# A two-layer transformer with experts: the triangular inversion on one engine, and operand tiles at multiples of 256 bytes

## The chip, the cores and the metric

The kernel is one program on one core of a Trainium2 chip. The metric is device microseconds of that core. Three runs of the kernel before took 2130.3, 2129.33 and 2136.47 us (median 2130.3). Engines: TensorE (PE in rows; PEld its weight loads), VectorE (DVE), ScalarE (ACT), GpSimd (POOL), SyncE (SP), which only issues transfers here. SBUF is the on-chip memory: a tile is a range of bytes at the same start address in each of the 128 partitions. For a matmul the stationary operand (the weights) is loaded first and the moving operand then streams past it.

## The reference

Two layers over 256 context and 256 latent tokens of width 1024, float32. Layer 0 mixes by bidirectional retention and grouped-query attention and has a dense SwiGLU of width 2816. Layer 1 mixes by differential attention and a bidirectional RWKV-7 recurrence and has eight SwiGLU experts of width 3584, two per token. The heavy matrix products and the recurrence, cut to what matters:

```python
def swiglu(h, wg, wu, wd):
    return (jax.nn.silu(h @ wg) * (h @ wu)) @ wd

# experts, layer 1: top 2 of 8, every expert's three matrices are read whole
for e in range(N_EXPERTS):
    out = out + gates[..., e:e + 1] * swiglu(h, wg[e], wu[e], wd[e])

# RWKV-7, one direction, per token
s_new = (s * wt[:, :, None, :]
         + jnp.einsum('bhvk,bhk->bhv', s, at)[..., None] * bt[:, :, None, :]
         + vt[..., None] * kt[:, :, None, :])
y = jnp.einsum('bhvk,bhk->bhv', s if read_before else s_new, rt)
```

## The kernel before

**Split matmuls.** Every weight matrix arrives in float32 and is split into a high half (a copy on ScalarE that rounds to float32r) and a low half (a subtraction on VectorE). One product is then three matmuls: high with high, high with low, low with high (`mm3`, L266 to 269). The split of weights is `wsplit` (L262 and 263: `raw` to `whi`, `wlo`) in the attention and dense parts and `split_to` (L272 and 273: `mraw` to `mhi`, `mlo`) in the expert part, where each transfer brings 1 MB. In the experts' gate and up products (`g`, `u`) the token tiles `xh`, `xl` are stationary and the weights `mhi`, `mlo` move; in the experts' down product (`y`) `acts` is stationary. In the dense FFN gate and up (`acc<-hTh,whi`) the weights are stationary and the tokens `hTh`, `hTl` move; in the dense down product (`acc<-whi,ah`) the activations `ah`, `al` are stationary. In the projections in front of attention (`acc<-whi,hTh`) the tokens are stationary.

**RWKV.** Time is cut into chunks of 64; each chunk and head needs the inverse of a unit lower triangular 64x64 matrix, done as two 32x32 diagonal inversions (`inv_blocks`, `inv_diag`) and a joining product (`inv_join`). All heads and chunks of one half (256 tokens, both directions) go at once, one per partition and block. `inv_blocks` lets TensorE build the blocks (`dg`, `off`) from the tiles `AR` and `BK` that `prep` computes on VectorE and ScalarE, and transposes them to `M`. `inv_diag` goes through 31 steps; step t multiplies column t of `M` by row t of the growing inverse `N` into a scratch tile, and adds it to `N` in place. VectorE has the columns below a cut (2 in half 0, 8 in half 1) with the scratch `tmv`, GpSimd the rest with `tmg`. `inv_join` transposes `N` twice into `X0` and `X1`, copies eight blocks into `XF` and computes the off-diagonal block by `gp` and `wp` on TensorE. `chain` then carries the state through the chunks with `lm`, `z`, `u`, `s` on TensorE and small copies on VectorE and ScalarE between.

**Order.** `weave` interleaves the issue of two sequences of steps in a given proportion: half 0's inversion beside `prep` of half 1, and half 1's inversion and join beside `chain` of half 0. Each engine works through its instructions in the order issued. Tiles come from pools; a pool's tiles are laid one behind the other, so a small tile ahead of large ones sets the address of all that follow. Weight transfers are issued by SyncE as far ahead as the ring of raw buffers allows.

Of the kernel before, what the change touches and what calls it, by code (L numbers as in the profile page):

```python
# [8 lines left out]
F32 = mybir.dt.float32  # L9
F32R = mybir.dt.float32r  # L10
I32 = mybir.dt.int32
# [14 lines left out]
LAM_INIT = 0.8 - 0.6 * math.exp(-0.3)  # L26
C = 64
RAW = 8

CUT0, CUT1 = 2, 8  # L30

NM, N0 = 72, 0.1
M1, M3 = 15, 1
# [97 lines left out]
def _build(top, tc, nc, V, S, G, T, I, O):  # L131
# [4 lines left out]
    def open_right(key, name, bufs=1):  # L136
        cur[key] = ExitStack()
        return cur[key].enter_context(tc.tile_pool(name=name, bufs=bufs, side="right", reuse_waits="tile"))
# [25 lines left out]
    acc, tpp, att, ybank = (bank(k) for k in ("acc", "tp", "at", "y"))  # L164
    banks(acc=range(6), tp=(6, 7))
    cur["re"] = cur["ce"] = ExitStack()
    top.callback(lambda: [cur[k].close() for k in ("we", "xe", "me", "he", "re", "ce")])

    def const_(shape, name, dt=F32):
        return cp.tile(shape, dt, name=name)  # L170
# [1 line left out]
    def load_consts(pool, g, queue=nc.scalar):  # L172
        t = pool.tile([128, CST["cst_" + g].shape[1]], F32, name="cst_" + g)
        queue.dma_start(t, I["cst_" + g])

        def cc(k):
            o, n = COFF[k]
            return t[:, o:o + n]
        return cc

    cc = load_consts(cp, "all")
    ident = cc("ident")

    Xl = const_([128, 2, D], "Xl")
    cur["rb"] = 4
    hp = cur["h"] = open_right("he", "h")
    hT = tuple(hp.tile([128, 8, 512], F32R, name=n_) for n_ in ("hTh", "hTl"))
    open_mod()
# [9 lines left out]
    def columns(name, parts):  # L198
# [4 lines left out]
        for nm, src, k in parts:  # L203
# [9 lines left out]
    voff = {}  # L213
    cvec = columns("cvec", (("c", I["c"].rearrange("o (k p) -> (o k) p", p=128), 8),
                            ("cc", I["c_ctx"].rearrange("(k p) -> k p", p=128), 8)))
    cond = const_([128, 8, 32], "cond")
    V.memset(cond, 0.0)
    S.activation(cond[:, :, 0:2].rearrange("p k r -> p r k"), cvec.rearrange("p (r k) -> p r k", r=2), AF.Silu)

# [571 lines left out]
    def layer1():  # L791
# [11 lines left out]
        mu1 = rp.tile([128, 15], F32, name="mu1")  # L803
        muh = rp.tile([128, 15], F32, name="muh")
        ka1 = rp.tile([128, 4], F32, name="ka1")
        o = voff["mu"]
        V.tensor_scalar(mu1, vec[:, o:o + 15], -1.0, 1.0, op0=ALU.mult, op1=ALU.add)
        V.tensor_scalar(muh, vec[:, o:o + 15], 0.5, None, op0=ALU.mult)
# [5 lines left out]
        twd = rp.tile([128, 512], F32, name="twd")  # L814
        adT = rp.tile([128, 512], F32, name="adT")
        sgd = rp.tile([128, 256], F32, name="sgd")
        bon = rp.tile([128, 2, 8], F32, name="bon")
        G.memset(vT[:, :, 0:64], 0.0)
        pads = []
        for i in range(2):  # L820
            p = xq.tile([128, 2, 258], F32, name=f"spad{i}")
            G.memset(p, 0.0)
            pads.append(p)

        def shift(i, a, dst, segs):

# [52 lines left out]
        def operands(pool, half):  # L879
            w = 64 * (1 + half)  # L880
            for d in range(2):
                AR[d, half] = pool.tile([128, 4, 4, w], F32, name=f"AR{d}{half}", tag=f"AR{d}{half}")
                BK[d, half] = pool.tile([128, 4, 4, 2, 64], F32, name=f"BK{d}{half}", tag=f"BK{d}{half}")
                WC[d, half] = pool.tile([128, 4, 4], F32, name=f"WC{d}{half}")

        def lora_weights(d):

# [131 lines left out]
            iv[half] = M, Lo  # L1019
            yield  # L1020

        def inv_diag(half, cut):

            M, Lo = iv[half]
            N = bn("N")
            G.memset(flat(N), 0.0)
            G.memset(flat(N)[:, 0:1024:33], 1.0)
            for t in range(31):
                for eng, name, j0, j1 in ((V, "tmv", 0, cut), (G, "tmg", cut, 31)):
                    j1 = min(j1, t + 1)  # L1030
                    if j1 <= j0:
                        continue
                    tm = qI.tile([128, 256], F32, name=name, tag=name, bufs=2)
                    n, m = 31 - t, j1 - j0
                    tv = tm[:, 0:n * m].rearrange("p (i j) -> p i j", i=n)
                    Nv = N[:, t + 1:32, j0:j1]
                    eng.tensor_tensor(tv, M[:, t + 1:32, t:t + 1].to_broadcast([128, n, m]),
                                      N[:, t:t + 1, j0:j1].to_broadcast([128, n, m]), op=ALU.mult)
                    eng.tensor_tensor(Nv, Nv, tv, op=ALU.add)
                yield  # L1040
            iv[half] = N, Lo
            yield

        def inv_join(half):

            N, Lo = iv[half]
            X0, X1 = bn("X0"), bn("X1")
            V.transpose(X0.rearrange("p u c -> p c u"), N.rearrange("p r c -> p c r"))
            V.transpose(X1.rearrange("p u r -> p r u"), N)
            yield  # L1050
            xf, xt = (X0, X1), (X1, X0)
            xF = XF[half].rearrange("p d c a t -> p d (c a) t")
            for d in range(2):
                for x in range(4):
                    V.tensor_copy(xF[32 * x:32 * x + 32, d, :, 32 * (x % 2):32 * (x % 2) + 32],
                                  xt[d][32 * x:32 * x + 32, 16 * d:16 * d + 16])
            gp = acc("gp")
            Gs = qI.tile([128, 16, 32], F32, name="Gs", tag="Gs", bufs=1)
            for d in range(2):
                for u in range(16):  # L1060
                    for h in range(2):
                        i_, o_ = 64 * h + 32 * d, 64 * h + 32 * (1 - d)
                        T.matmul(gp[o_:o_ + 32, u * 32:u * 32 + 32], Lo[i_:i_ + 32, u], xf[d][i_:i_ + 32, 16 * d + u],
                                 start=True, stop=True, tile_position=(i_, o_))
            S.activation(flat(Gs), gp, AF.Copy)
            yield
            wp_ = acc("wp")
            for d in range(2):
                for u in range(16):
                    for h in range(2):  # L1070
                        o_, i_ = 64 * h + 32 * d, 64 * h + 32 * (1 - d)
                        T.matmul(wp_[o_:o_ + 32, u * 32:u * 32 + 32], Gs[i_:i_ + 32, u], xt[d][i_:i_ + 32, 16 * d + u],
                                 start=True, stop=True, tile_position=(i_, o_))
            for d in range(2):
                for h in range(2):
                    o_ = 64 * h + 32 * d
                    S.activation(xF[o_:o_ + 32, d, :, 32 * (1 - d):32 * (1 - d) + 32],
                                 wp_[o_:o_ + 32].rearrange("p (u t) -> p u t", u=16), AF.Copy)
            yield

        banks(acc=(3, 4, 5), at=(0, 1, 2))
        drain(inv_blocks(0))
        weave((seq(prep(0, 1), prep(1, 1), inv_blocks(1)), 19), (inv_diag(0, CUT0), 32))
        rk = q.tile([128, 4, 256], F32, name="rkT", tag="Ei", bufs=1)
        for p in range(4):
            V.scalar_tensor_tensor(rk[:, p], rT[:, p], vcol("rk", p), kT[:, p, 256:512], op0=ALU.mult, op1=ALU.mult)
# [128 lines left out]
                ops.update(nxt)  # L1215
                yield

        weave((chain(0), 16), (seq(inv_diag(1, CUT1), inv_join(1)), 32))
        eI.close()
        eC.close()  # L1220
        mh, ml = (qA.tile([128, 8, 256], F32R, name=n_, tag=t_) for n_, t_ in (("mixh", "BK00"), ("mixl", "BK10")))
# [231 lines left out]
    def moe():  # L1453
# [3 lines left out]
        top_e, mp = top_pool("moe")  # L1457
        mc = load_consts(mp, "moe", nc.sync)
        h2h = {}
        h2l = mp.tile([128, 2, D], F32R, name="h2l")  # L1460
        Ar, Br, rt, rb = cur["route"]
        sel = mp.tile([128, 2, NE], F32, name="sel")
        gts = mp.tile([128, 2, NE], F32, name="gts")
        slotv = mp.tile([128, 2, NE], F32, name="slotv")
        wg, wu, wd = I["moe_w_gate"][0], I["moe_w_up"][0], I["moe_w_down"][0]
        split = []

# [153 lines left out]
        def gate_weights():  # L1621
# [13 lines left out]
            V.tensor_copy(cnt, ct[:, 0:8])  # L1635
            V.tensor_reduce(cm_, ct[:, 0:8], axis=AX.X, op=ALU.max)
            V.tensor_copy(cmx, cm_)
        cnt = mp.tile([128, NE], I32, name="cnt")
        cmx = mp.tile([128, 1], I32, name="cmx")


        def gather(g, k2s=range(4)):
# [240 lines left out]
```

## Time and profile before

| what | value |
|---|---|
| median of three runs | 2130.3 us |
| profiled execution | 2132.66 us, span 2130.9 us |
| TensorE busy | 2038.5 us (96%), mean granted clock 0.973 |
| VectorE busy | 1646.4 us (77%) |
| ScalarE busy | 1210.4 us (57%) |
| GpSimd busy | 152.6 us (7%) |
| bytes moved | 494.00 MB, mean 232 GB/s |

The profile is of one execution. Busy time is the time in which an engine works on some instruction; TensorE's matmuls are pipelined, so that two of them overlap and their durations add up to more than its busy time. How closely matmuls follow each other is read from the distance of their starts. The granted clock is the share of full speed (2.4 GHz) at which TensorE was let run. The idle time in front of an instruction is put down to what released it.

### The profile page before, as it was taken

To read this page: it belongs to the slowest core of one execution; us is meant where nothing else is said; L and a number is where in the kernel's file an instruction comes from. 1 tells how busy PE (TensorE), PEld (TensorE's weight loads), DVE (VectorE), ACT (ScalarE), POOL (GpSimd) and SP (SyncE) were. 2 spreads that over 40 slices of the span, in tenths; PEclk is the share of its full clock that TensorE was granted. 3 is DMA by queue.
4 is the path that set the end of the run, shared out by engine and by line. 5 is a ranking of instruction groups with operands and counts; after the bars stand their busy time and mean duration, and the time that the engine had idled before them with its cause. 6 is when DMAs were issued, how large, how long until landed. Compare 5 with 4: busy or idle time off the path is not lost. (4 is left out here: it accounts for less than half of the span.)

```text
span 2130.9 us, 30220 instructions
## 1 busy us (share of the span) xinstructions
PE 2038.5 (96%) x11649; PEld 1621.1 (76%) x11650; DVE 1646.4 (77%) x2083; ACT 1210.4 (57%) x1557; POOL 152.6 (7%) x211
## 2 busy tenths in 40 slices
PE   7999989999999899869989999999999999999997
PEld 2767778878788666758877888888788787888875
DVE  3967793675556657687579999889989899889987
ACT  3543343222234445632348777777777777777775
POOL 0211110000000110184010000000000000000000
PEclk9999999999999999977899999999999999999999
DMA  8535352466645331100197999999999999999993
GB/s 299 163 106 169 105 175 60 149 229 206 190 157 188 102 90 55 34 19 12 62 333 267 361 307 362 337 352 360 349 347 341 352 376 353 334 356 361 360 352 143
DMA packets 224203, 494.00 MB, mean 232 GB/s; under 512 B 11355, under 2 KB 45262, under 8 KB 224054
## 3 DMA queue, kind: packets, MB, share of 16 engines
q1 hardware_dynamic: 219968, 482.62, 65.0%
q10 hardware_dynamic: 4086, 9.40, 1.3%
q8 instruction: 93, 1.52, 0.3%
q14 instruction: 56, 0.46, 0.1%
HBM read 490.87 MB, written 1.11 MB: 231 GB/s over the span
## 5 line engine op out<-in xcount | busy, mean ns | idle before, releaser
L273 DVE TENSOR_TENSOR mlo<-mraw,mhi 128x1024 fp32r<-128x1024 f32 x668 | 789.0, 1220 | 79.4 <-ACT mhi L272 62.6
L272 ACT ACTIVATE mhi<-mraw 128x1024 fp32r<-128x1024 f32 x668 | 683.3, 1057 | 106.6 <-PE y L269 49.0
L262 ACT ACTIVATE whi<-raw 128x1024 fp32r<-128x1024 f32 (+1 forms) x150 | 152.9, 1023 | 276.3 <-PE acc L269 108.8
L263 DVE TENSOR_TENSOR wlo<-raw,whi 128x1024 fp32r<-128x1024 f32 (+1 forms) x146 | 172.7, 1186 | 136.0 <-ACT whi L262 135.5
L267 PE MATMUL acc<-hTh,whi 128*128 128x512 f32 (+1 forms) x504 | 190.6, 380 | 0.0
L268 PE MATMUL acc<-hTl,whi 128*128 128x512 f32 (+1 forms) x504 | 186.6, 371 | 0.0
L269 PE MATMUL acc<-hTh,wlo 128*128 128x512 f32 (+1 forms) x504 | 185.7, 369 | 0.0
L268 PE MATMUL g<-mlo,xh 128*128 128x512 f32 x448 | 182.4, 407 | 0.0
L337 DVE SCALAR_TENSOR_TENSOR part<-mraw,cond,part 128x1024 f32<-128x1024 f32 x112 | 149.8, 1358 | 41.9 <-DMA mraw<-in_mod_w 41.7
L267 PE MATMUL g<-mhi,xh 128*128 128x512 f32 x448 | 178.7, 399 | 0.0
L267 PE MATMUL u<-mhi,xh 128*128 128x512 f32 x448 | 177.4, 396 | 0.0
L268 PE MATMUL u<-mlo,xh 128*128 128x512 f32 x448 | 177.3, 396 | 0.0
L269 PE MATMUL u<-mhi,xl 128*128 128x512 f32 x448 | 177.1, 395 | 0.0
L269 PE MATMUL g<-mhi,xl 128*128 128x512 f32 x448 | 177.1, 395 | 0.0
L268 PE MATMUL y<-mlo,acts 128*128 128x512 f32 x448 | 175.8, 392 | 0.3 <-DVE mlo L273 0.3
L269 PE MATMUL y<-mhi,acts 128*128 128x512 f32 x448 | 174.8, 390 | 0.0
L267 PE MATMUL y<-mhi,acts 128*128 128x512 f32 x448 | 151.4, 390 | 0.0
L268 PE MATMUL acc<-wlo,hTh 128*128 128x512 f32 x336 | 135.1, 402 | 4.5 <-DVE wlo L263 4.5
L267 PE MATMUL acc<-whi,hTh 128*128 128x512 f32 x336 | 135.8, 407 | 3.4 <-ACT whi L262 2.0
L269 PE MATMUL acc<-whi,hTl 128*128 128x512 f32 x336 | 134.0, 400 | 0.0
L267 PEld LDWEIGHTS acc<-hTh,whi 128*128 128x128 f32 x504 | 95.4, 190 | 22.5 <-issue 4.1
L268 PEld LDWEIGHTS acc<-hTl,whi 128*128 128x128 f32 x504 | 95.0, 189 | 17.6 <-issue 2.8
(433 smaller groups left out, 3378.3 us busy)
## 6 DMA issues: line engine op xcount, KB each, us to landing
mraw<-in_moe_w_gate SPq DMA_DIRECT2D x112, 1024.0 KB
mraw<-in_moe_w_up SPq DMA_DIRECT2D x112, 1024.0 KB
mraw<-in_moe_w_down SPq DMA_DIRECT2D x110, 1024.0 KB
mraw<-in_mod_w SPq DMA_DIRECT2D x96, 512.0 KB
raw<-in_ffn_w_down SPq DMA_DIRECT2D x32, 512.0 KB
raw<-in_odd_w_in SPq DMA_DIRECT2D x26, 512.0 KB
raw<-in_even_w_in SPq DMA_DIRECT2D x24, 512.0 KB
raw<-in_ffn_w_gate SPq DMA_DIRECT2D x20, 512.0 KB
```

Of the source, the lines that this page charges most:

```text
L262: S.activation(h, v, AF.Copy)
L263: (eng or V).tensor_tensor(l, v, h, op=ALU.subtract)
L267: T.matmul(out, ah, bh, start=first, stop=False)
L268: T.matmul(out, ah, bl, start=False, stop=False)
L269: T.matmul(out, al, bh, start=False, stop=last)
L272: S.activation(hi, src, AF.Copy)
L273: eng.tensor_tensor(lo, src, hi, op=ALU.subtract)
L337: V.scalar_tensor_tensor(part[r], w, c_, part[r], op0=ALU.mult, op1=ALU.add)
```

## The change

Three edits.

1. `inv_diag` loses its cut: all columns of a step are on VectorE in one multiplication and one addition, and the scratch `tmg` and GpSimd's share go.
2. In `inv_join` four of the eight copies into `XF` are issued to ScalarE.
3. Padding tiles (`pad_`) of 128 to 224 bytes are put in front of the large tiles of several pools, and a few small tiles (`cond`, `bon`, `WC`, `cnt`, `cmx`, `h2l`) change place, so that the large tiles start at multiples of 256 bytes.

```diff
+    def pad_(pool, nbytes, name):
+        pool.tile([128, nbytes // 4], F32, name=name)
+    pad_(cp, 160, "lpad")
...
+    pad_(open_right("pe", "edge"), 224, "edge")
...
-    cond = const_([128, 8, 32], "cond")
+    cond = cur["m"].tile([128, 8, 32], F32, name="cond")
...
+        pad_(rp, 160, "rwpad")
+        pad_(xq, 192, "shpad")
+            pad_(pool, 128, f"wcpad{half}")
...
-                for eng, name, j0, j1 in ((V, "tmv", 0, cut), (G, "tmg", cut, 31)):
...
+                tm = qI.tile([128, 256], F32, name="tmv", tag="tmv", bufs=2)
+                n, m = 31 - t, t + 1
+                tv = tm[:, 0:n * m].rearrange("p (i j) -> p i j", i=n)
+                Nv = N[:, t + 1:32, 0:m]
+                V.tensor_tensor(tv, M[:, t + 1:32, t:t + 1].to_broadcast([128, n, m]),
+                                N[:, t:t + 1, 0:m].to_broadcast([128, n, m]), op=ALU.mult)
+                V.tensor_tensor(Nv, Nv, tv, op=ALU.add)
...
-                    V.tensor_copy(xF[32 * x:32 * x + 32, d, :, 32 * (x % 2):32 * (x % 2) + 32],
-                                  xt[d][32 * x:32 * x + 32, 16 * d:16 * d + 16])
+                    (S.copy if x % 2 else V.tensor_copy)(xF[32 * x:32 * x + 32, d, :, ...],
+                                                         xt[d][32 * x:32 * x + 32, 16 * d:16 * d + 16])
...
-        h2l = mp.tile([128, 2, D], F32R, name="h2l")
...
+        cnt = mp.tile([128, NE], I32, name="cnt")
+        cmx = mp.tile([128, 1], I32, name="cmx")
+        pad_(mp, 224, "mpad")
+        h2l = mp.tile([128, 2, D], F32R, name="h2l")
```

Start addresses of the operands of split matmuls in the two programs, modulo 256 bytes:

| product | before: moving / stationary | after |
|---|---|---|
| experts' gate and up (`mhi`, `mlo` / `xh`, `xl`) | 64 / 128 | 0 / 0 |
| experts' down (`mhi`, `mlo` / `acts`) | 64 / 64 | 0 / 0 |
| layer 0's projections (`whi`, `wlo` / `hTh`, `hTl`) | 224 / 224 | 0 / 0 |
| dense FFN gate and up (`hTh`, `hTl` / `whi`, `wlo`) | 224 / 224 | 0 / 0 |
| dense FFN down (`whi`, `wlo` / `ah`, `al`) | 224 / 96 | 0 / 0 |
| layer 1's diff projection (`whi`, `wlo` / `hTh`, `hTl`) | 160 / 224 | 0 / 0 |
| layer 1's RWKV projection (`hTh`, `hTl` / `whi`, `wlo`) | 224 / 160 | 0 / 0 |
| layer 1's output projection (`whi`, `wlo` / `mixh`, `mixl`) | 64 / 96 and 160 | 0 / 0 |

The tiles that transfers fill move too: `mraw` of the expert ring and `raw` from 224 to 0, `mraw` of the experts' borrowed places from 64 to 0, the modulation's `mraw` from 224 to 0; `fc`, which holds the RWKV gains, was and is at 0.

**GpSimd in half 0.** Before, behind the clearing of `N`, GpSimd's queue holds a product and a sum for each step (sizes in elements per partition):

```order
L889 MEMSET w2p 64x512
L1026 MEMSET N 128x1024
L1027 MEMSET N 128x32
L1037 TENSOR_TENSOR tmg<-M,N 128x29
L1039 TENSOR_TENSOR N<-N,tmg 128x29
L1037 TENSOR_TENSOR tmg<-M,N 128x56
L1039 TENSOR_TENSOR N<-N,tmg 128x28x2
L1037 TENSOR_TENSOR tmg<-M,N 128x81
```

After, the same place:

```order
L898 MEMSET w2p 64x512
L1035 MEMSET N 128x1024
L1036 MEMSET N 128x32
L899 MEMSET a2p 64x512
L1127 MEMSET UV 64x512 x4
L1035 MEMSET N 128x1024
L1036 MEMSET N 128x32
L1127 MEMSET UV 64x512 x12
```

The products and sums are gone; clearing `N` is followed by clearing two small tiles and by half 1's `N`.

**VectorE in half 0, around the second direction's `AR`.** This tile (from `kk` and `Ee`) is what TensorE's `dg` of half 1 waits for. Before:

```order
L1039 TENSOR_TENSOR N<-N,tmv 128x16x2
L1037 TENSOR_TENSOR tmv<-M,N 128x30
L1039 TENSOR_TENSOR N<-N,tmv 128x15x2
L962 TENSOR_TENSOR BK_6855<-tb,En 128x16x64
L1037 TENSOR_TENSOR tmv<-M,N 128x28
L963 TENSOR_TENSOR AR_6854<-kk,Ee 128x16x64
L1039 TENSOR_TENSOR N<-N,tmv 128x14x2
L967 TENSOR_TENSOR tb<-kT,at 128x1024
L1037 TENSOR_TENSOR tmv<-M,N 128x26
L970 COPY WC_6856<-Ei 128x16
L968 TENSOR_TENSOR BK_6855<-tb,En 128x16x64
L1039 TENSOR_TENSOR N<-N,tmv 128x13x2
```

After:

```order
L975 TENSOR_SCALAR at<-at,vec,ka_5385 128x256
L1042 TENSOR_TENSOR tmv<-M,N 128x240
L1044 TENSOR_TENSOR N<-N,tmv 128x20x12
L1042 TENSOR_TENSOR tmv<-M,N 128x247
L971 TENSOR_TENSOR BK_6865<-tb,En 128x16x64
L1044 TENSOR_TENSOR N<-N,tmv 128x19x13
L972 TENSOR_TENSOR AR_6864<-kk,Ee 128x16x64
L1042 TENSOR_TENSOR tmv<-M,N 128x252
L976 TENSOR_TENSOR tb<-kT,at 128x1024
L1044 TENSOR_TENSOR N<-N,tmv 128x18x14
L977 TENSOR_TENSOR BK_6865<-tb,En 128x16x64
L1042 TENSOR_TENSOR tmv<-M,N 128x255
```

Before, the `AR` row stands behind the product of step 17 (28 elements, two columns); after, behind the sum of step 12 (13 columns). The inversion's rows ahead of it are 35 before and 26 after, the rest stands behind it.

**VectorE at the join of half 0.** Before, two transposes and eight copies stand between the inversions of half 0 and half 1:

```order
L1048 STREAM_TRANSPOSE X_7608<-N 128x32x32
L1049 STREAM_TRANSPOSE X_7609<-N 128x32x32
L1055 COPY XF_6860<-X_7608 32x16x32
L1055 COPY XF_6860<-X_7609 32x16x32 x4
L1055 COPY XF_6860<-X_7608 32x16x32 x3
L1037 TENSOR_TENSOR tmv<-M,N 128x31
L1039 TENSOR_TENSOR N<-N,tmv 128x31
```

After:

```order
L1053 STREAM_TRANSPOSE X_7530<-N 128x32x32
L1054 STREAM_TRANSPOSE X_7531<-N 128x32x32
L1060 COPY XF_6869<-X_7530 32x16x32
L1060 COPY XF_6869<-X_7531 32x16x32 x2
L1060 COPY XF_6869<-X_7530 32x16x32
L1042 TENSOR_TENSOR tmv<-M,N 128x31
L1044 TENSOR_TENSOR N<-N,tmv 128x31
```

Four copies are left; the other four stand in ScalarE's queue, ahead of half 1's `Lo`.

## Rows read from the trace of the kernel before

**Rows 1.** The page's engines: busy us, share of the span, x instructions.

```profile
PE 2038.5 (96%) x11649; PEld 1621.1 (76%) x11650; DVE 1646.4 (77%) x2083; ACT 1210.4 (57%) x1557; POOL 152.6 (7%) x211
```

**Rows 2.** Windows: length, busy us by engine, granted clock, DMA share, GB/s.

```profile
500.00:600.00 100.00, 100.00 (x441) 80.14 (x440) 58.95 (x60) 28.45 (x36) 4.00 (x6) 1.00 0.66 208
900.00:1000.00 100.00, 81.25 (x1367) 70.78 (x1367) 77.78 (x181) 34.31 (x59) 64.65 (x115) 0.71 0.06 18
1400.00:1500.00 100.00, 100.00 (x447) 81.23 (x446) 90.65 (x84) 78.36 (x83) 0.00 (x0) 1.00 0.99 360
```

**Rows 3.** Waits of SyncE's DMA queue: who waits for whom, total us, times, longest.

```profile
SPq L1420 <- DVE mlo L273: 814.6, 318, 7.7
```

**Rows 4.** Timeline of TensorE, experts' gate/up: start us, duration us, line, operands.

```profile
1501.55 0.39 PE L268 MATMUL u<-mlo,xh 128*128 128x512 f32 x1
...
1505.51 0.40 PE L267 MATMUL g<-mhi,xh 128*128 128x512 f32 x1
```

**Rows 5.** Timeline of TensorE, experts' down product.

```profile
2085.12 0.39 PE L269 MATMUL y<-mhi,acts 128*128 128x512 f32 x1
...
2087.16 0.39 PE L269 MATMUL y<-mhi,acts 128*128 128x512 f32 x1
```

**Rows 6.** Timeline of TensorE, dense FFN gate/up.

```profile
560.15 0.39 PE L267 MATMUL acc<-hTh,whi 128*128 128x512 f32 x1
...
565.59 0.39 PE L267 MATMUL acc<-hTh,whi 128*128 128x512 f32 x1
```

**Rows 7.** Timeline of TensorE, dense FFN down.

```profile
640.22 0.39 PE L267 MATMUL acc<-whi,ah 128*128 128x512 f32 x1
...
645.79 0.39 PE L267 MATMUL acc<-whi,ah 128*128 128x512 f32 x1
```

**Rows 8.** Timeline of TensorE, diff projection of layer 1.

```profile
745.22 0.39 PE L267 MATMUL acc<-whi,hTh 128*128 128x512 f32 x1
...
749.41 0.39 PE L267 MATMUL acc<-whi,hTh 128*128 128x512 f32 x1
```

**Rows 9.** The page's groups: line, engine, operands, shapes, count, busy us, mean ns, idle.

```profile
L273 DVE TENSOR_TENSOR mlo<-mraw,mhi 128x1024 fp32r<-128x1024 f32 x668 | 789.0, 1220 | 79.4 <-ACT mhi L272 62.6
...
L267 PE MATMUL g<-mhi,xh 128*128 128x512 f32 x448 | 178.7, 399 | 0.0
...
L267 PE MATMUL y<-mhi,acts 128*128 128x512 f32 x448 | 151.4, 390 | 0.0
```

**Rows 10.** Groups by form, TensorE, 380 to 700 us.

```profile
L267 PE MATMUL acc<-hTh,whi 128*128 128x512 f32 x258 | 101.3, 393 | 0.0
...
L267 PE MATMUL acc<-whi,ah 128*128 128x512 f32 x176 | 69.9, 397 | 0.0
```

**Rows 11.** Groups by form, TensorE, 0 to 300 us.

```profile
L267 PE MATMUL acc<-whi,hTh 128*128 128x512 f32 x256 | 103.7, 408 | 2.3 <-ACT av L579 1.1 <-ACT whi L262 0.9 <-ACT hTh L272 0.3
```

**Rows 12.** Windows of the inversion, half 0 and half 1.

```profile
906.28:957.66 51.38, 33.92 (x536) 29.05 (x535) 45.40 (x98) 19.63 (x31) 43.62 (x64) 0.77 0.07 19
...
965.70:1005.00 39.30, 38.51 (x724) 34.90 (x725) 27.12 (x93) 11.50 (x23) 14.30 (x35) 0.75 0.05 15
```

**Rows 13.** Groups by line, VectorE, 906.28 to 957.66 us.

```profile
L1037 DVE TENSOR_TENSOR tmv<-M,N 128x31 f32<-128x31 f32 (+30 forms) x31 | 12.0, 386 | 0.6
...
L1114 DVE TENSOR_TENSOR Lm<-lm,cst_rwkv 128x256 f32<-128x256 f32 x5 | 2.1, 419 | 4.4 <-PE lm L1111 4.4
```

**Rows 14.** Groups by line, VectorE, 965.7 to 1005 us.

```profile
L1037 DVE TENSOR_TENSOR tmv<-M,N 128x112 f32<-128x112 f32 (+29 forms) x31 | 9.0, 291 | 0.7
```

**Rows 15.** Timeline of VectorE, half 1 of the inversion.

```profile
983.38 0.33 DVE L1037 TENSOR_TENSOR tmv<-M,N 128x184 f32<-128x184 f32 x1
```

**Rows 16.** Waits between 906 and 1005 us.

```profile
PE dg L1008 <- DVE AR L963: 8.7, 1, 8.7
```

**Rows 17.** DMA queues, 948 to 954 us: packets, MB, share of 16 engines.

```profile
q10 hardware_dynamic: 432, 0.79, 42.2%
```

**Rows 18.** DMA queues, 1400 to 1500 us.

```profile
q1 hardware_dynamic: 14494, 35.91, 98.4%
```

More of the change, by code (lines that the diff above doesn't have):

```diff
@@ L28 @@
 RAW = 8
-CUT0, CUT1 = 2, 8
 NM, N0 = 72, 0.1
@@ L166, in _build @@
     cur["re"] = cur["ce"] = ExitStack()
-    top.callback(lambda: [cur[k].close() for k in ("we", "xe", "me", "he", "re", "ce")])
+    top.callback(lambda: [cur[k].close() for k in ("we", "xe", "me", "he", "re", "ce", "pe")])
     def const_(shape, name, dt=F32):
@@ L185, in _build @@
     cur["rb"] = 4
+    cur["pe"] = ExitStack()
+    pad_(open_right("pe", "edge"), 224, "edge")
     hp = cur["h"] = open_right("he", "h")
@@ L805, in layer1 @@
         ka1 = rp.tile([128, 4], F32, name="ka1")
+        bon = rp.tile([128, 2, 8], F32, name="bon")
+        pad_(rp, 160, "rwpad")
         o = voff["mu"]
@@ L816, in layer1 @@
         sgd = rp.tile([128, 256], F32, name="sgd")
-        bon = rp.tile([128, 2, 8], F32, name="bon")
         G.memset(vT[:, :, 0:64], 0.0)
@@ L881, in operands @@
             for d in range(2):
+                WC[d, half] = pool.tile([128, 4, 4], F32, name=f"WC{d}{half}")
+            pad_(pool, 128, f"wcpad{half}")
+            for d in range(2):
                 AR[d, half] = pool.tile([128, 4, 4, w], F32, name=f"AR{d}{half}", tag=f"AR{d}{half}")
                 BK[d, half] = pool.tile([128, 4, 4, 2, 64], F32, name=f"BK{d}{half}", tag=f"BK{d}{half}")
-                WC[d, half] = pool.tile([128, 4, 4], F32, name=f"WC{d}{half}")
         def lora_weights(d):
@@ L1020, in inv_blocks, with inv_diag @@
             yield
-        def inv_diag(half, cut):
+        def inv_diag(half):
             M, Lo = iv[half]
@@ L1028, in inv_diag @@
             for t in range(31):
-                for eng, name, j0, j1 in ((V, "tmv", 0, cut), (G, "tmg", cut, 31)):
[L1030 to L1039, printed above, removed]
+                tm = qI.tile([128, 256], F32, name="tmv", tag="tmv", bufs=2)
[5 more added lines that the diff above has]
+                V.tensor_tensor(Nv, Nv, tv, op=ALU.add)
                 yield
@@ L1054, in inv_join @@
                 for x in range(4):
-                    V.tensor_copy(xF[32 * x:32 * x + 32, d, :, 32 * (x % 2):32 * (x % 2) + 32],
-                                  xt[d][32 * x:32 * x + 32, 16 * d:16 * d + 16])
+                    (S.copy if x % 2 else V.tensor_copy)(xF[32 * x:32 * x + 32, d, :, 32 * (x % 2):32 * (x % 2) + 32],
+                                                         xt[d][32 * x:32 * x + 32, 16 * d:16 * d + 16])
             gp = acc("gp")
@@ L1082, in layer1 @@
         drain(inv_blocks(0))
-        weave((seq(prep(0, 1), prep(1, 1), inv_blocks(1)), 19), (inv_diag(0, CUT0), 32))
+        weave((seq(prep(0, 1), prep(1, 1), inv_blocks(1)), 19), (inv_diag(0), 32))
         rk = q.tile([128, 4, 256], F32, name="rkT", tag="Ei", bufs=1)
@@ L1216, in chain @@
                 yield
-        weave((chain(0), 16), (seq(inv_diag(1, CUT1), inv_join(1)), 32))
+        weave((chain(0), 16), (seq(inv_diag(1), inv_join(1)), 32))
         eI.close()
@@ L1637, in gate_weights @@
             V.tensor_copy(cmx, cm_)
-        cnt = mp.tile([128, NE], I32, name="cnt")
-        cmx = mp.tile([128, 1], I32, name="cmx")
         def gather(g, k2s=range(4)):
```

## The prediction

> **What bounds the kernel now.** I read the busy times first: TensorE is busy in 2038.5 of 2130.9 us [rows 1], so the time can change by much only if TensorE's own stream gets shorter or one of its few gaps does. Second the windows: in 500 to 600 us (dense FFN) and 1400 to 1500 us (experts) TensorE is at 100.00 of 100 at a granted clock of 1.00, while from 900 to 1000 us (the inversion) it is at 81.25 and the clock at 0.71 [rows 2]. In the expert window VectorE stands at 90.65 and the DMA share at 0.99: two resources close behind the first. Third the DMA queue's waits: SyncE waits 814.6 us for buffers that VectorE's low half frees [rows 3], so the transfers are held back by the consumers there.
>
> Last the timelines of the split matmuls, start to start, because durations overlap (they read 0.39 us at any spacing). The reader is to take the first and last start and divide by the intervals between. Gate/up of the experts: 1501.55 to 1505.51 is 3.96 us over 17 intervals, 232.9 ns [rows 4]. The experts' down product: 2085.12 to 2087.16, 2.04 over 9, 226.7 ns [rows 5]. Dense FFN gate/up: 560.15 to 565.59, 5.44 over 24, 226.7 ns [rows 6]. Dense FFN down: 640.22 to 645.79, 5.57 over 24, 232.1 ns [rows 7]. Diff projection: 745.22 to 749.41, 4.19 over 18, 232.8 ns [rows 8]. All five are 128x128 by 512 columns of the same type at full clock, with no idle between. What sorts them is the pair of start addresses, modulo 256, in the table of the change: equal for moving and stationary operand (64/64, 224/224) in the two at 226.7, unequal (64/128, 224/96, 160/224) in the three at 232 to 233. The number of intervals is the number of matmul rows between the two shown. This is a correlation over five places, not a proof; the change makes all pairs equal.
>
> **The change part by part.** *Addresses, the experts.* Gate and up run six groups of 448 matmuls [rows 9], 2688. Going from 232.9 to 226.7 saves 6.2 ns each, 16.7 us. The experts' down product (3 x 448) is already at the equal pitch: 0. Behind TensorE are VectorE and the DMA: saving 16.7 of about 1000 us of expert time (1.7%) raises VectorE from 90.65 to 92.2 and the need of bytes from 360 GB/s by 6 GB/s [rows 2]. Neither is full, but both have stretches with less room than the mean, so I take three quarters of it, 12.5 us; bounds 0 (the cover is gone) and 16.7. VectorE's low half at 1.22 us x 668 [rows 9] is 815 us and is taken to stay.
>
> *Addresses, elsewhere.* Dense FFN down: 3 x 176 [rows 10] x 5.4 ns = 2.9 us, TensorE being the bound there. Diff projection: about 240 matmuls x 6.1 ns = 1.5 us. The remaining unequal products of layer 1 (about 340 matmuls, which I estimate at half of 6 ns as they are partly waiting for their operands) 1 us. Together 5.4; bounds 0 and 7. The products already at equal addresses, dense gate/up (258 x 3 in one window) [rows 10] and layer 0's (256 x 3) [rows 11], are set to 0: the equal address moves from 224 to 0, which no row shows for these operands; from below their bound is 213 ns (512 columns at 2.4 GHz), from above the 233 of the unequal ones. I take 226.7 since 64 and 224 gave the same to the tenth.
>
> The padding tiles issue nothing. The conditioning tile and the bonus tile only change their place in memory.
>
> *The inversion, half 0.* From 906.28 to 957.66 VectorE is busy 45.40 of 51.38 us and GpSimd 43.62 [rows 12]. VectorE's 2 x 31 instructions of the first two columns cost 2 x 12 us at a mean of 386 ns [rows 13], though they hold at most 60 elements. In half 1, where GpSimd is busy only 14.30 of 39.30 us [rows 12], an instruction with up to eight columns takes 291 ns [rows 14]. One of 184 elements takes 0.33 us there [rows 15] and one of 1024 takes 1.220 [rows 9]: 1.06 ns an element and 0.135 us fixed. All 31 columns are sums of (31-t)(t+1) = 5456 elements for each of the two operations: 2 x (31 x 0.135 + 5456 x 0.00106) = 19.9 us. So the whole work costs VectorE less (19.9) than a part of it did beside GpSimd (24), and GpSimd's part goes. What waits there is TensorE, for the second direction's AR tile, 8.7 us [rows 16]. By the order that AR stands behind 35 of the inversion's instructions before and behind 26 now. 35 x 0.386 us are 13.5; 26 x 0.135 + 4186 x 0.00106 are 7.9: it comes 5.6 us sooner, at most 8.7. After it 36 instructions with 6726 elements remain, 12.0 us against 27 x 0.386 = 10.4, in a stretch where VectorE idles 4.4 us for TensorE before its Lm products [rows 13], which covers the 1.6. I take 5 us.
>
> *Half 1.* Some 18 us of VectorE (2 x 9.0) become 19.9 and up to 22 with the gaps between dependent instructions; it is beside the chunk chain, where TensorE is busy 38.51 of 39.30 us and VectorE 27.12 [rows 12]. The 12 us of room cover 2 to 4; if the cover were gone it would cost 4. Queued behind each inversion instruction are the copies that the chain waits for, delayed by at most one of 0.4 us; six chunks of them, at worst 3 us.
>
> *Four of eight copies to ScalarE.* They leave VectorE between its two transposes and the joining products; ScalarE is busy 19.63 of 51.38 us in half 0 [rows 12] and takes them at once. Gain and cost 0, either way at most 2 us.
>
> For the inversion as a whole I take -5 us. Bounds: +8 (both half 1's delays on the path) and -14 (the granted clock, 0.77 in the first window and 0.75 in the next, with TensorE busy 33.92 and 38.51 us, giving back most of what it lost there). The value is nearest to the row of the AR wait, the one gap of TensorE that it touches.
>
> **The sum.** 12.5 + 5.4 + 5 = 22.9 us. The profiled execution took 2132.66 us, 1.76 more than its span: 2109.8. The median of the runs is 2130.3, 2.4 below the profiled one: 2107.
>
> **Two rules of the Trainium skill, weighed.** The rows give two spacings, 226.7 and 232 to 233, for one shape. "SBUF — State Buffer", section "Who interferes with whom", says that TensorE reads its moving operand and its weights through two independent ports; by it the relation of two addresses could not matter, and the sum would be the inversion's 5 us alone. The rows disagree in their numbers but name no cause, so this is a rival below. The other rule speaks for more: "DMA: Bandwidth & Descriptors", section "How a descriptor splits into AXI transactions", has a descriptor that starts off a 256-byte boundary pay an extra transaction. An estimate from that page: 64 beats instead of 71 for 2 KB, 10% less. In rows, packets into a tile already at residue 0 took 42.2% of 16 x 6 us over 432, 94 ns, under a light load [rows 17]; expert packets into tiles at 224 and 64 took 98.4% of 16 x 100 us over 14494, 109 ns, at full load [rows 18]. Loads differ, so they don't decide. By that rule the expert stage would keep all of the 16.7 us, and the time would be 2103.
>
> **The rivals.**
> *Only the inversion counts (2125; 2116 to 2138).* The spacing follows something else that differs between the five places (which operand is the weights, how long it has been in memory), and equal addresses leave it at 232.9. For it: five places are few. Against: dense down and dense gate/up read the same ring of weight tiles at 224 and differ in the other operand's address.
> *Better than equal (2073).* Residue 0 lets matmuls go at 213 ns: 2688 x 19.6 + (1344 + 768 + 774) x 13.4 + 768 x 18.8 = 106 us, of which the room on VectorE (9 of 100) and the DMA lets about half through, so -57 with the inversion's part (the 774 are the dense gate/up of rows 10, the last 768 dense down and diff). For it: no operand of these was at 0 so far. Against: two different residues gave 226.7 to the tenth.
> *Slower (2143).* A common residue of 0 makes weights, moving operand, VectorE's and ScalarE's writes and the arriving packets start in the same place of memory, and all split matmuls take the longer spacing: the 2886 at equal addresses at +6.2 ns, 18 us, less 5 for the inversion: +13. It decides when the mean spacing of all split matmuls is over 230.8 ns, where what the products at equal addresses lose eats what the others and the inversion gain. Against: the experts' down product, with both operands at 64 and 360 GB/s arriving, takes the shorter one.
>
> **How the numbers follow.** Forecast 0.57 (its own range 2096 to 2118), only the inversion 0.20, better than equal 0.14, slower 0.09. About 0.3% (6.4 us) is what a measurement of this kernel can tell from no change. The forecast lies beyond it nearly always (0.55); of the second case 0.05 is faster and 0.13 the same, 0.02 slower; all of the third is faster; of the last 0.01 is the same. With the forecast's 0.02: faster 0.74, same 0.16, slower 0.10. The range 2080 to 2130 leaves out the far part of the third case, the last case and the slow end of the second.
>
> **What the changed profile would show.** Right: gate/up, dense down and diff start every 227 ns, the experts' period is some 2 us shorter, half 0's VectorE instructions cost 0.145 to 0.41 us, and TensorE's wait for AR is near 3 us. TensorE still at 100 in the expert windows says that nothing else took over; a gap there behind the low half or a packet says that the cover was used up. Wrong: gate/up still at 233 (addresses don't matter), the experts' down product off 226.7 in either direction (residue 0 differs from 64), or a TensorE wait in half 1 for copies behind inversion instructions.

## The result, and the profile after

The changed kernel takes 2110.86 us (median of four runs, 2107.18 to 2112.08) against 2131.4 us (four runs of the kernel before). The ratio is 0.9896, with a 95% interval of 0.9879 to 0.9913: about 20.5 us less. Forecast were 2107 us in a range of 2080 to 2130, and faster with a chance of 0.74.

The engines of the page after, as in [rows 1]:

```profile
PE 2018.4 (96%) x11649; PEld 1620.8 (77%) x11650; DVE 1637.6 (78%) x2075; ACT 1214.5 (58%) x1563; POOL 93.4 (4%) x107
```

TensorE's busy time fell by 20.1 us, from 2038.5 to 2018.4, which is nearly the whole gain: its own stream got shorter. GpSimd's fell by 59 us; at 4% of the span it bounds nothing by itself.

Three windows of the kernel after (length, busy us of each engine, granted clock, DMA share, GB/s), as in [rows 2]:

```profile
500.00:600.00 100.00, 100.00 (x443) 80.40 (x442) 59.15 (x61) 29.43 (x37) 4.54 (x7) 1.00 0.66 210
900.00:1000.00 100.00, 85.69 (x1468) 76.70 (x1469) 82.77 (x206) 35.80 (x65) 7.50 (x15) 0.75 0.08 24
1400.00:1500.00 100.00, 100.00 (x450) 82.00 (x449) 91.50 (x86) 77.66 (x84) 0.00 (x0) 1.00 0.99 366
```

In the dense and expert windows TensorE is at 100.00 of 100 as before, so nothing took its place as the bound; short waits of its weight loads don't show in this number and come up below. More matmuls fit into them (450 against 447), VectorE rose from 90.65 to 91.50 and the bytes from 360 to 366 GB/s. The window around the inversion went from 81.25 to 85.69.

The timeline of TensorE after (start us, duration us, line, operands), first and last row of an unbroken stretch, where [rows 4 to 8] were read. Line numbers of the product are 5 higher than before. Experts' gate and up, 32 intervals:

```profile
1539.71 0.40 PE L273 MATMUL g<-mlo,xh 128*128 128x512 f32 x1
...
1546.99 0.39 PE L272 MATMUL u<-mhi,xh 128*128 128x512 f32 x1
```

Experts' down product, 26 intervals:

```profile
2087.03 0.39 PE L273 MATMUL y<-mlo,acts 128*128 128x512 f32 x1
...
2092.92 0.39 PE L273 MATMUL y<-mlo,acts 128*128 128x512 f32 x1
```

Dense FFN gate and up, 32 intervals:

```profile
544.64 0.39 PE L272 MATMUL acc<-hTh,whi 128*128 128x512 f32 x1
...
551.89 0.39 PE L274 MATMUL acc<-hTh,wlo 128*128 128x512 f32 x1
```

Dense FFN down, 32 intervals:

```profile
637.67 0.39 PE L273 MATMUL acc<-wlo,ah 128*128 128x512 f32 x1
...
644.92 0.39 PE L272 MATMUL acc<-whi,ah 128*128 128x512 f32 x1
```

Diff projection, 32 intervals:

```profile
731.67 0.39 PE L274 MATMUL acc<-whi,hTl 128*128 128x512 f32 x1
...
738.93 0.39 PE L273 MATMUL acc<-wlo,hTh 128*128 128x512 f32 x1
```

Divided out: 227.5, 226.5, 226.6, 226.6 and 226.9 ns. The two spacings of before have become one; the three places at 232 to 233 moved, the two at 226.7 stayed.

The windows of the inversion after, from the first inversion instruction of half 0 to the first transpose behind it, the join up to half 1's first instruction, and half 1, as in [rows 12]:

```profile
901.52:951.35 49.83, 40.51 (x563) 35.40 (x562) 41.51 (x98) 19.26 (x32) 2.54 (x6) 0.74 0.07 20
951.45:956.64 5.19, 3.09 (x113) 3.09 (x115) 5.14 (x7) 2.47 (x4) 0.92 (x2) 0.50 0.01 3
956.64:997.40 40.76, 39.30 (x760) 35.87 (x754) 32.03 (x99) 12.63 (x26) 3.94 (x8) 0.79 0.06 18
```

Half 0 takes 49.83 us instead of 51.38 and TensorE does more in it (40.51 against 33.92), the join 5.19 instead of 8.04. VectorE's groups in half 0, as in [rows 13]:

```profile
L1044 DVE TENSOR_TENSOR N<-N,tmv 128x31 f32<-128x31 f32 (+15 forms) x31 | 10.6, 341 | 0.5
L1042 DVE TENSOR_TENSOR tmv<-M,N 128x31 f32<-128x31 f32 (+15 forms) x31 | 10.5, 340 | 0.6
```

62 instructions with all 31 columns cost 21.1 us, less than the first two columns alone did beside GpSimd.

What TensorE waits for between 900 and 1000 us after, as in [rows 16]:

```profile
PE gp L1068 <- DVE X L1053: 3.6, 2, 2.3
PE dg L1017 <- DVE AR L972: 2.5, 2, 1.4
```

The wait for `AR` went from 8.7 to 2.5 us. A new one came in its place: `gp`, the joining product, now waits 3.6 us for VectorE's transposes, since TensorE arrives there with nothing else to do.

Where the 21.55 us between the two profiled executions' spans went, from the starts of the same instructions in both traces: 4.7 up to the end of dense down (of which 3.1 between its first and last matmul), 1.7 in the diff projection, -1.6 in the RWKV projection, 3.9 from the inversion's first instruction to the chain's last `u`, 0.2 up to the first expert matmul, 12.3 from there to the last one, 0.3 behind it. The parts up to the RWKV projection come from one pair of profiles, and other profiles of the same addresses differ by as much. The experts' 12.3 us is firmer: that stage takes 984.6 to 985.0 us in all five profiles with the experts' operands at 0, and 997.0 in both with the old addresses.

### The profile page after: what moved, and what is told of

The parts are those of the page before. It is cut to its first block, busy times and chain, and to the rows that moved or that the text cites. A ratio compares the mean times of both kernels' runs of the same rounds, so it can differ in the third digit from the quotient of the medians.

```text
span 2109.4 us, 30113 instructions
## 1 busy us (share of the span) xinstructions
PE 2018.4 (96%) x11649; PEld 1620.8 (77%) x11650; DVE 1637.6 (78%) x2075; ACT 1214.5 (58%) x1563; POOL 93.4 (4%) x107
```

## The experiments

The edits are small; all but the first stand on the changed kernel. Times are medians; in each comparison the kernel before ran on the same chip (2131.26, 2132.74 and 2133.5 us in the three groups of four). The change itself did not run again in these groups, so against its 2110.86 us a difference of 2 or 3 us in the medians says little; the length of the expert stage (start of its first gate to start of its last down matmul), 984.75 us in the change and 997.03 before, is the steadier measure there.

**The inversion alone**, at the old addresses.

```diff
-                for eng, name, j0, j1 in ((V, "tmv", 0, cut), (G, "tmg", cut, 31)):
+                n, m = 31 - t, t + 1          # all columns on VectorE, as in the change
-                    V.tensor_copy(xF[...], xt[d][...])
+                    (S.copy if x % 2 else V.tensor_copy)(xF[...], xt[d][...])
```

> The kernel before with the inversion on VectorE alone and four copies on ScalarE, all tiles at their old addresses. My theory: the inversion is worth about 4 us and the addresses the rest, so 2127 us (2125 to 2129), and gate/up of the experts stay at 233 ns from start to start. Rival: the padding has nothing to do with it and the whole gain of 20.5 us comes from the inversion's stage, then 2111 us. Second rival: the inversion on VectorE alone is worth nothing by itself, since TensorE is nearly full beside it, then 2131 us.

Measured: 2127.17 us, ratio 0.9981 (0.9971 to 0.9991), 4.1 us less. The first theory holds; gate/up stayed at 233.4 to 233.9 ns, and TensorE's wait for `AR` is 2.5 us as in the change.

**The addresses alone**, with the inversion and the copies of before.

```diff
-        weave((seq(prep(0, 1), prep(1, 1), inv_blocks(1)), 19), (inv_diag(0), 32))
+        weave((seq(prep(0, 1), prep(1, 1), inv_blocks(1)), 19), (inv_diag(0, CUT0), 32))
```

> The changed addresses with the inversion as before (columns shared by VectorE and GpSimd, eight copies on VectorE). My theory: 2115 us (2113 to 2117), all split matmuls of 512 columns at 226.7 ns, and this saving and that of the inversion alone add up to the whole within 2 us. Rival: the two halves overlap (VectorE's room in the expert stage cannot matter for the inversion, but the clock could): then this one alone is within 1 us of the whole change.

Measured: 2114.66 us, ratio 0.992 (0.9906 to 0.9933), 16.6 us less. The wait for `AR` is 8.2 us, nearly that of before. The parts add: 4.1 + 16.6 = 20.7 against 20.5 for the whole, closer than their intervals (2 to 3 us each way) can show.

**The stationary operand at 64, the moving one at 0.**

```diff
             e, q = top_pool("ex")
+            pad_(q, 64, "xpad")
```

> The changed kernel with 64 bytes in front of the experts' token tiles: the stationary operand of gate and up lies at 64 modulo 256, the moving one stays at 0, the down product stays at 0 and 0. Theory that the pair must be equal: gate and up go back to 232.9 ns, down stays at 226.7, and what the expert stage gained (12.3 us from the first gate matmul to the last down matmul in the profiles) goes, so 2123 us (2121 to 2125). Theory that each operand off a 256-byte boundary costs its own part: 230 ns and 2117 us. Theory that addresses don't matter for the spacing: 2111 us.

Measured: 2122.55 us, ratio 0.9962 (0.9949 to 0.9976): 64 bytes of padding in front of two tiles, and so of what lies behind them in the pool, cost 11.7 us; the expert stage is back at 996.90 us. The timeline, 25 intervals of 233.2 ns:

```profile
1541.11 0.39 PE L274 MATMUL g<-mhi,xl 128*128 128x512 f32 x1
...
1546.94 0.39 PE L272 MATMUL g<-mhi,xh 128*128 128x512 f32 x1
```

**All of the experts' operands at 64.**

```diff
-        pad_(mp, 224, "mpad")
+        pad_(mp, 288, "mpad")
```

> The changed kernel with all operands of the experts' matmuls (high and low halves, token tiles, activations) at 64 modulo 256 instead of 0; the ring of raw buffers stays at 0. Theory that the pair must be equal: spacing 226.7 ns and 2111 us (2109 to 2113). Theory that a multiple of 256 itself counts: gate and up at 233 ns or above and 2123 us, more if the down product follows.

Measured: 2109.65 us, ratio 0.9905 (0.9889 to 0.992), not to be told from the change. A multiple of 256 is not what counts; that the two agree is.

**The moving operand at 64, the stationary one at 0.**

```diff
-        pad_(mp, 224, "mpad")
+        pad_(mp, 288, "mpad")
...
             e, q = top_pool("ex")
+            pad_(q, 192, "xpad")
```

> The changed kernel with the experts' high and low halves and activations at 64 modulo 256 and the token tiles at 0: the pair of gate and up is 64 and 0, of the down product 64 and 64. Theory that the pair must be equal: the mirror image of the run with the token tiles at 64, so gate and up at 233 ns, down at 226.7, 2123 us (2121 to 2125). Rival, that only the stationary operand must lie at a multiple of 256 (its loads are short, so a split costs them more): gate and up at 226.7 ns, 2111 us, and the down product at 233.

Measured: 2113.5 us, ratio 0.9915 (0.99 to 0.993). Both theories fail: unequal, yet only 2.6 us slower than the change, 2.9 us in the expert stage, and 32 intervals of 229.1 ns:

```profile
1539.66 0.40 PE L274 MATMUL g<-mhi,xl 128*128 128x512 f32 x1
...
1546.99 0.39 PE L273 MATMUL u<-mlo,xh 128*128 128x512 f32 x1
```

So the pair 64/0 is not the mirror image of 0/64. (That a load off a multiple of 256 is split is the rival's supposition; no run shows one.) What was left to ask was whether the stationary operand counts for itself or the signed difference does.

**The stationary operand at 32.** (As the third edit, with 32.)

> The changed kernel with 32 bytes in front of the experts' token tiles, so the pair of gate and up is 0 and 32. Theory that the residues modulo 256 must be the same: 233 ns and 2123 us as with 64 bytes. Rival, that the two starts must share a unit of 64 bytes: 226.7 ns and 2111 us. Anything between would mean that the size of the difference counts: 230 ns and 2117 us.

Measured: 2122.36 us, ratio 0.9958 (0.9944 to 0.9972), 31 intervals of 233.2 ns:

```profile
1509.66 0.40 PE L274 MATMUL u<-mhi,xl 128*128 128x512 f32 x1
...
1516.89 0.40 PE L272 MATMUL g<-mhi,xh 128*128 128x512 f32 x1
```

**The ring of raw buffers at 224.**

```diff
+        pad_(open_right("px", "rpad"), 32, "rpad")
         rq = open_right("ce", "mraw")
```

> The changed kernel with the ring of eight raw buffers, into which 288 of the experts' 336 chunks arrive, at 224 modulo 256 as it was before; all operands of matmuls stay at 0. My theory: transfers and ScalarE's and VectorE's reads don't care for the address, 2111 us (2109 to 2113), and packets of the expert stage take the same 109 ns or so. Rival: unaligned packets take up to 10% longer and the expert stage, whose DMA share is 0.99, gives back 4 us or more, so 2115 us or above.

Measured: 2109.53 us, ratio 0.9901 (0.9885 to 0.9917): no loss. The DMA queue from 1400 to 1500 us (packets, MB, share of 16 engines), first of the change with the ring at 0, then with the ring at 224:

```profile
q1 hardware_dynamic: 14805, 36.52, 98.6%
```

```profile
q1 hardware_dynamic: 14838, 36.58, 99.3%
```

98.6% of 1600 us over 14805 packets are 106.6 ns, 99.3% over 14838 are 107.1. These durations hold waiting too, so by themselves they don't exclude a small cost; but the expert stage takes 984.62 us against 984.75, so none reaches the time.

**Half 1 of the inversion shared again.**

```diff
-        weave((chain(0), 16), (seq(inv_diag(1), inv_join(1)), 32))
+        weave((chain(0), 16), (seq(inv_diag(1, 8), inv_join(1)), 32))
```

> The changed kernel with half 0's inversion on VectorE alone, but half 1's shared as before (eight columns on VectorE, the rest on GpSimd). Theory that half 1 is covered by the chunk chain: 2111 us (within 1 us). Rival: VectorE's 21 instead of 18 us there delay the chain's copies, so sharing gives 2 to 3 us back, 2108 us. Third: GpSimd's half of the work slows VectorE beside it and the chain is later, 2113 us.

Measured: 2113.04 us, ratio 0.9912 (0.9899 to 0.9926), which is 2 us above the change with intervals that overlap. Half 1's inverse is done 8 us sooner; VectorE's first instruction and transpose in this kernel, then in the change:

```profile
952.63 0.27 DVE L1046 TENSOR_TENSOR tmv<-M,N 128x31 f32<-128x31 f32 x1
...
984.92 2.06 DVE L1057 STREAM_TRANSPOSE X<-N 128x1024 f32<-128x1024 f32 x1
```

```profile
956.64 0.20 DVE L1042 TENSOR_TENSOR tmv<-M,N 128x31 f32<-128x31 f32 x1
...
997.40 2.06 DVE L1053 STREAM_TRANSPOSE X<-N 128x1024 f32<-128x1024 f32 x1
```

That is 32.3 against 40.8 us, and from the first instruction of half 1 to the chain's last `u` it is still 99 us in both (952.63 to 1051.7, 956.64 to 1055.5). In these two profiles half 1 is covered. The profile of this run is of its fastest execution (2107.95 us), 5 us under the median. The median is the number of the third theory, but its cause, a later chain, does not show; that sharing gains nothing is shown, that it costs 2 us is not.

**The stationary operand at 192**, the moving one at 0. (As the third edit, with 192.)

> The changed kernel with the experts' token tiles (stationary) at 192 modulo 256, the moving operands of gate and up at 0. So far gate/up took 227.3 ns at 0/0 and 64/64 (moving/stationary), 229.0 at 64/0, 233.4 at 0/64 and 233.3 at 0/32. Theory of the difference: the spacing depends on stationary minus moving modulo 256; here it is 192, the same as in the run with 64/0, so 229 ns and 2113 to 2115 us. Theory of the stationary operand: it alone must lie at a multiple of 256 (or at the residue of the moving one), then 233 ns and 2122 us.

Measured: 2113.88 us, ratio 0.9906 (0.9891 to 0.9921), 31 intervals of 228.7 ns:

```profile
1509.77 0.39 PE L273 MATMUL u<-mlo,xh 128*128 128x512 f32 x1
...
1516.86 0.39 PE L274 MATMUL u<-mhi,xl 128*128 128x512 f32 x1
```

The theory of the difference holds here: 0 - 64 and 192 - 0 are the same modulo 256 and give the same, with the stationary operand at a multiple of 256 in one and off it in the other.

**The stationary operand at 224.** (As the third edit, with 224.)

> The same with the token tiles at 224. Theory of the difference: 224 is nearer to a whole 256 than 192, so 227.5 to 229 ns and 2111 to 2114 us. Theory of the stationary operand: 233 ns and 2122 us, as 32 bytes the other way gave.

Measured: 2120.28 us, ratio 0.9934 (0.9921 to 0.9948), 31 intervals of 233.2 ns:

```profile
1533.77 0.39 PE L274 MATMUL u<-mhi,xl 128*128 128x512 f32 x1
...
1541.00 0.39 PE L272 MATMUL g<-mhi,xh 128*128 128x512 f32 x1
```

Both numbers of the theory of the difference are missed here, and the theory of the stationary operand, which missed in the run before, meets both of its own (233 ns, 2122 us). Neither stands as it was written. What fits both runs is that the difference decides, with no rule for how: that nearness to 256 helps is wrong.

**The stationary operand at 128.** (As the third edit, with 128.)

> The same with the token tiles at 128. Theory of the difference: the dense down product before the change (moving 224, stationary 96, difference 128) took 232.1 ns, so the same here and 2119 to 2121 us. Theory of the stationary operand: 233.4 ns and 2122 us. The two are close here; the run fills the curve between 64 and 192.

Measured: 2121.53 us, ratio 0.9941 (0.9928 to 0.9955), 31 intervals of 232.3 ns. It can't tell the two theories apart, and was not expected to; it agrees with the dense down product before [rows 7].

**The copies into XF on VectorE.**

```diff
-                    (S.copy if x % 2 else V.tensor_copy)(xF[...], xt[d][...])
+                    V.tensor_copy(xF[...], xt[d][...])
```

> The changed kernel with all eight copies into XF back on VectorE. They stand between the two transposes of the inverse and the joining products. Theory that they are hidden: 2111 us, within 1 us. Rival: in the changed kernel TensorE has a gap at the join (busy 3.09 of the 5.19 us from the first transpose's start to half 1's first inversion instruction), so 1 to 2 us per half come back on the path and it takes 2112 to 2114 us.

Measured: 2116.3 us, ratio 0.9916 (0.9903 to 0.993). Compared by ratios with the change (0.9896) it is some 4 us slower, with intervals that overlap a little. The windows of this kernel, half 0's join and half 1:

```profile
951.13:958.09 6.96, 4.22 (x131) 4.08 (x131) 6.85 (x10) 1.09 (x2) 0.92 (x2) 0.50 0.01 2
958.09:1000.58 42.49, 41.89 (x749) 37.66 (x750) 32.03 (x99) 12.60 (x25) 3.94 (x8) 0.78 0.07 22
```

The join takes 6.96 us instead of 5.19 and half 1 42.49 instead of 40.76 in the profiles. The rival is the better one; the size is not settled to better than 2 to 5 us. Beside the addresses alone (0.992) this also says that VectorE's inversion without the copies (0.9916) gains nothing that the times can tell. The profiles say where it goes: from the first inversion instruction to the chain's first `u` it is 71.0 us before, 70.7 with the addresses alone, 64.6 in the change and 64.5 here, so half 0's gain needs no copies; from the first to the last `u` it is 86.9, 89.4, 89.4 and 92.9, so it is beside half 1 that they count. These are single profiles, and the last stretch lies between 87.5 and 90.2 in the other runs of the changed inversion. Both stretches together take 157.4 us here, 160.1 with the addresses alone, and 151.0 to 154.1 in the nine profiles with the new addresses, VectorE's inversion and the copies shared.

Together, the mean spacing of `u` in each profile (start to start within the product, 200 to 300 ns, some 1209 distances each), the expert stage and the median:

| stationary minus moving, modulo 256 | pairs run (moving/stationary) | ns | expert stage, us | median, us |
|---|---|---|---|---|
| 0 | 0/0, 64/64 | 227.3, 227.1 | 984.75, 984.72 | 2110.86, 2109.65 |
| 32 | 0/32 | 233.3 | 996.49 | 2122.36 |
| 64 | 64/128 (before, all else old too), 0/64 | 233.4, 233.4 | 997.03, 996.90 | 2131.4, 2122.55 |
| 128 | 0/128 | 232.9 | 995.91 | 2121.53 |
| 192 | 64/0, 0/192 | 229.0, 229.0 | 987.63, 987.79 | 2113.5, 2113.88 |
| 224 | 0/224 | 233.3 | 996.50 | 2120.28 |

Differences of 0, 64 and 192 were each seen at two pairs in these profiles. That it is the remainder modulo 256 which counts rests on the row of 192, where the plain differences are -64 and 192. Other products of the kernel before agree: diff (difference 64) 233.3 ns, dense down (128, as 224/96) 232.4, the RWKV projection (192) 229.3, layer 1's output projection (32 and 96) 232.1. In the change they are at 227.1 to 227.9.

None of the runs beats the change by more than these measurements can tell.

## Why the prediction was right, and where its steps were off

*What bounds the kernel: right.* TensorE's stream was the bound, and it got shorter by what the time lost.

*The spacing is a matter of the two addresses: right, and now shown* by an edit of 64 bytes that gives back 11.7 us and by one that moves all of the experts' operands alike and gives back nothing. The Trainium skill ("SBUF — State Buffer", section "Who interferes with whom") calls TensorE's two read ports independent; by that, as the prediction applied it, the third run would have taken 2111 us, and it took 2122.55. *"Unequal costs 6 ns" was too coarse:* the unequal places that it rests on had differences of 64, 128 and 64, and at 192 the loss is 1.7 ns. The RWKV projection of the kernel before, with 192, was at 229.3 ns and would have shown it; its spacing was not read.

*Experts' gate and up, 12.5 us: measured 12.3. The reason holds for a part of the shortfall, and that three quarters came so close is luck.* I took three quarters of 16.7 us because VectorE or the DMA would have too little room in places. The expert stage from its first gate to its last down matmul, before and after:

```profile
1117.33:2114.36 997.03, 996.59 (x4483) 807.49 (x4482) 894.39 (x864) 764.38 (x823) 2.41 (x1) 1.00 0.94 340
```

```profile
1108.40:2093.15 984.75, 984.26 (x4482) 806.09 (x4482) 891.44 (x864) 765.44 (x823) 2.41 (x1) 1.00 0.94 344
```

TensorE is idle for 0.4 and 0.5 us of it, and its own waits there sum to 0.3 us in both. What is missing lies in the `g` product: from `u` to `u` 1212 distances sum to 283.23 us before and 275.95 after, 6.0 ns each; from `g` to `g` 1179 distances sum to 282.36 and 278.76, 3.05 ns each. In 49 stretches of `g` the transposes of the activations stand between the matmuls. These take 3.04 us on average before and 3.05 after, while in the other stretches of `g` 667 distances went from 233.4 to 227.1 ns. Twelve matmuls at 6.2 ns that were not saved and 18 ns that were lost, 49 times, are 4.5 us, about the whole shortfall.

Part of its cause stands in the trace. Distances over 300 ns in `g` went from 71 to 91, and at each of the 20 new ones the weight load in front of the matmul waits for VectorE's low half. One such place, before and after, with what ScalarE and VectorE do ahead of it after:

```profile
1552.32 0.19 PEld L268 LDWEIGHTS g<-mlo,xh 128*128 128x128 f32 x1 [0.30 <-DVE mlo L273]
```

```profile
1534.18 0.60 ACT L1692 ACTIVATE msg<-g 128x512 f32<-128x512 f32 x1 [1.66 <-PE g L274]
...
1535.76 1.23 DVE L278 TENSOR_TENSOR mlo<-mraw,mhi 128x1024 fp32r<-128x1024 f32 x1 [1.24 <-ACT mhi L277]
...
1537.04 0.19 PEld L273 LDWEIGHTS g<-mlo,xh 128*128 128x128 f32 x1 [0.37 <-DVE mlo L278]
```

ScalarE's `msg` (the silu of `g`) waits for the last `g` matmul of the round before, the next high half stands behind it in ScalarE's queue, and VectorE's low half waits for that one. From that last `g` matmul to the waiting one it is 3.29 us at all 20 places in both kernels, so what the matmuls in between saved went into the wait: the matmul behind it starts 339 ns after the one in front, before it was 257. That is 82 ns 20 times, 1.6 us. So at these places the cover was used up before the change already: the weight loads of `g` wait 6.3 us for `mlo` in the profile before and 7.9 after. The prediction guessed this from the shares of VectorE and the DMA; the waits of the weight loads would have given the places. Why the other distances around the transposes fell only to 231.2 ns (409 of them) was not tried and stays open.

*Elsewhere, 5.4 us: some 4.6 by the spacings.* Dense down went from 232.4 to 227.1 ns, 2.8 us over its 528 matmuls, forecast 2.9; diff from 233.3 to 227.5, 1.4 us over 240, forecast 1.5; the output projection brings 0.4. The stages' lengths can't check this: from the first to the last `acc<-whi,ah`, with gate and up in between, it is 254.84 us before and 251.75 after, but 251.5 to 254.8 over all runs at the new addresses and 254.8 and 258.0 at the old ones. The RWKV projection gave nothing (116.9 us from first to last start before, 116.8 to 117.1 in all other profiles but the change's and one more, which show 118.5): with a difference of 192 it had little to lose.

*The inversion, 5 us: measured 4.1 alone and 3.8 as the difference of the addresses alone to the whole, copies included.* VectorE's 19.9 us for one half came out as 21.1 (the shortest step, 31 elements, takes 0.19 us; the 0.145 us of the forecast is too low even by its own line, which gives 0.168); `AR` came and TensorE's wait for it fell by 6.2 us, forecast 5.6. That the time came out near 5 us is partly luck: with all copies on VectorE the same shorter wait brought nothing that the times can tell. The cover of the remaining instructions was less good than thought, as this timeline of VectorE after shows:

```profile
941.80 0.38 DVE L1042 TENSOR_TENSOR tmv<-M,N 128x207 f32<-128x207 f32 x1
945.64 0.42 DVE L1119 TENSOR_TENSOR Lm<-lm,cst_rwkv 128x256 f32<-128x256 f32 x1 [3.46 <-PE lm L1116]
945.98 0.36 DVE L1044 TENSOR_TENSOR N<-N,tmv 128x207 f32<-128x207 f32 x1
```

An `Lm` stands in VectorE's queue and waits 3.46 us for TensorE's `lm`; behind it wait the inversion's last steps, and behind those `gp` on TensorE. VectorE's idle time in front of its `Lm` in half 0 was 4.4 us before [rows 13] and is 4.7 after, so none of it served as cover. Half 1's inverse itself is covered, as costed: done 8 us sooner, it did not end the chain sooner.

*The copies, 0 at most 2 either way: too low, as far as the runs show.* By the ratios they are worth about 4 us, with intervals that overlap a little, and that is all that the inversion's part brought in the times: half 0's 6 us came, and without the copies half 1 and the chain took most of them back in the one profile. The prediction put the term at 0 because ScalarE has room, and did not ask what TensorE does at the join. Before, it was busy throughout:

```profile
957.66:965.70 8.04, 8.04 (x86) 6.03 (x86) 7.85 (x10) 2.33 (x4) 6.73 (x18) 0.50 0.01 2
```

In the changed kernel it is busy for 3.09 of 5.19 us there and waits for the transposes.

*The rivals.* "Only the inversion" gave its 4.1 us and no more. "Better than equal" did not come: 0/0 and 64/64 are the same. "Slower" neither. The rule on split descriptors ("DMA: Bandwidth & Descriptors", section "How a descriptor splits into AXI transactions", of the Trainium skill) has no trace here: packets of 107.1 and 106.6 ns, an expert stage of 984.62 against 984.75 us, and 2109.53 against 2110.86 us.

## What to carry to other kernels

Read the distance of matmul starts, not their durations, and compare places of equal shape: where they differ by a few per cent and nothing waits, the operands' addresses are a candidate, and a padding tile of 64 bytes is the experiment. Make the moving and the stationary operand start at the same place modulo 256; it needn't be 0 (shown for 128x128 by 512 columns of this type). A faster engine gains nothing in a stretch whose length a chain through other engines sets; look for such waits at the weight loads too, not only at the matmuls. Before a small piece of work on VectorE is called hidden, look whether the change makes its stretch the place where TensorE waits.

## What was not expected

The spacing depends on the signed difference: 229.0 ns at 192, reached from either side, but 233.3 at 224 and at 32. What in the chip makes 0 best and 192 second was not found. VectorE's 31 products of 2 to 60 elements took 386 ns on average while GpSimd worked beside them on the same tiles, and 31 products of 31 to 256 elements 340 ns without it; one of 60 elements took 0.22 us then.
